# State-space branch in finer pipelined steps: half swaps on ScalarE, rotation tables on VectorE, one Toeplitz tile

## The chip, the cores and the metric

The kernel runs on one core of a Trainium2 chip. A core has five engines with a queue each: TensorE (PE: matmuls, with its weight loads PEld), VectorE (DVE), ScalarE (ACT), GpSimd (POOL) and SyncE (SP, which issues all transfers of this kernel). The metric is the device time of one execution in microseconds (us).

## The reference, cut to what matters

A decoder block on 1,024 tokens and 16 prepended ones (1,040 rows, width 1,024): one input projection, a state-space branch (S5) and a differential attention branch that are merged by gates, an output projection, and a feed-forward part with a convolution. The part that is changed computes, for 32 groups of 16 channels with 64 complex states each:

```python
x_re = jnp.einsum('blgc,gpc->blgp', ug, bb_re)
x_im = jnp.einsum('blgc,gpc->blgp', ug, bb_im)
_, _, s_re, s_im = lax.associative_scan(combine, (a_re_t, a_im_t, x_re, x_im), axis=1)
y = (jnp.einsum('blgp,gcp->blgc', s_re, c_re)
     - jnp.einsum('blgp,gcp->blgc', s_im, c_im) + d * ug)
```

The state obeys s[t] = a s[t-1] + x[t] with a complex a for each group and state.

## The kernel before, in words

Time is cut into 130 chunks (NJ) of 8 steps (CH). Inside a chunk the 8 steps are handled by matmuls: a Toeplitz matrix of the 8 lags (`Tz`, 128x128 for each group) from input to output, a matrix `VB` from input to the chunk's state, and `CL` from state to output. From chunk to chunk the state is a rotation times a decay. The rotation is taken out with tables of cosine and sine (`COS`, `SIN`, 130 columns per group), so that a real scan with the decay is left. The 32 groups go in four batches of 8 (`GB`). The 128 partitions hold 64 real and 64 imaginary parts, so turning a complex number needs a copy with the two halves exchanged (`Vs` of `Vv`, `zs` of `z`).

`ssm()` is a generator. It first computes small parameters on VectorE (three steps), and then each batch in four steps: (1) load the input `U` and the parameters, build the tables by doubling on GpSimd (`COS`, `SIN`, scratch `rot`: 8 rounds of 6 operations), and make `Z` on VectorE; (2) make `CL`, transpose `Z` into `VB`, multiply for the lag matrix `KM`, zero `Tn` on GpSimd, place `KM` into `Tn` by 8 transfers (L672), and reorder `Tn` into `Tz` by a ScalarE copy; (3) `vps = VB x U` evicted by ScalarE into `Vv`, the swap `Vs` by two transfers, turn, eight scans into `z` (L691), the swap `zs` by two transfers, turn back into `zp`; (4) `yps = CL x zp + Tz x U`, evicted and stored.

These steps are traced between the blocks of the input projection: four steps, then one before each of 12 blocks (query, key and value of four heads), and the rest (three yields) each with fillers. A block is three chunks of 348, 346 and 346 columns with 24 matmuls each. For queries and keys a norm follows: ScalarE squares the chunk into `qv` and copies it to `qraw`, and then `norm` (put into `self.later`) multiplies `qv` by a block matrix (`qss`, in the only PSUM buffer of tag `q`) and finishes on VectorE and ScalarE. `run_later` runs the waiting norms after the next chunk's matmuls.

Fillers are the 16 gate blocks and the two output matmuls of the state-space branch, handed out in items of three matmuls; an item is priced 3 x columns / 2400 us. Each of the remaining `ssm` yields takes items until PRE = 9 us are spent. What is left goes into the attention, where PE keeps the traced order and `pump(us)` calls dose the items; what remains at the end is issued at once. Gate 14 also starts `load_y`, which brings the branch's output back for its gelu.

Outside the attention the order on each engine is set when the kernel is built, by a planner that runs the instructions on a simulated time line. `keep_in_program_order(ins)` puts an instruction behind the one that was traced before it on the same engine; what is traced later may still be issued ahead of it. Each engine then works its list in order.

## Time and profile before

| | |
|---|---|
| runs | 1458.82, 1459.75, 1461.63 us (median 1459.75) |
| profiled execution | 1459.82 us, span 1458.0 us, mean granted clock 0.988 |
| PE busy | 1414.3 us (97%) |
| DVE, ACT, POOL busy | 1031.1, 613.5, 508.8 us |
| input projections with the state-space batches | about 60 to 300 us |
| attention | about 300 to 652 us |
| output projection and feed-forward | from about 652 us |

A view of waits shows for an engine's line what it waited for, the total, how often and the longest. A view of windows shows busy time in a stretch, the number of instructions, and PEclk, the clock granted to TensorE as a share of 2.4 GHz. A line can be that of a helper: L92 is `tt`, L104 is `act`, L130 and L182 are the matmuls of projections and fillers.

### The profile page before, as it was taken

To read this page: it belongs to the slowest core of one execution; us is meant where nothing else is said; L and a number is where in the kernel's file an instruction comes from. 1 tells how busy PE (TensorE), PEld (TensorE's weight loads), DVE (VectorE), ACT (ScalarE), POOL (GpSimd) and SP (SyncE) were. 2 spreads that over 40 slices of the span, in tenths; PEclk is the share of its full clock that TensorE was granted. 3 is DMA by queue.
4 is the path that set the end of the run, shared out by engine and by line. 5 is a ranking of instruction groups with operands and counts; after the bars stand their busy time and mean duration, and the time that the engine had idled before them with its cause. 6 is when DMAs were issued, how large, how long until landed. Compare 5 with 4: busy or idle time off the path is not lost.

```text
span 1458.0 us, 23036 instructions
## 1 busy us (share of the span) xinstructions
PE 1414.3 (97%) x8714; PEld 1301.7 (89%) x8714; DVE 1031.1 (71%) x1902; ACT 613.5 (42%) x1144; POOL 508.8 (35%) x453
## 2 busy tenths in 40 slices
PE   7979999999999999999999999999999999999998
PEld 7979898999999888999999899998899998788887
DVE  7958677645646869557565998888676768896574
ACT  6133343335545477443244543333333333444442
POOL 2085574511111311000122056666555566231030
PEclk9999999999999989999999999999999999999999
DMA  5424334382423523558434313334233236944331
GB/s 196 137 67 127 107 109 117 125 218 61 117 87 117 132 74 90 195 166 311 136 121 141 112 62 123 123 126 136 95 108 109 95 123 217 366 161 154 125 126 58
DMA packets 78206, 195.72 MB, mean 134 GB/s; under 512 B 9360, under 2 KB 21008, under 8 KB 78096
## 3 DMA queue, kind: packets, MB, share of 16 engines
q1 hardware_dynamic: 78096, 194.26, 41.4%
q8 instruction: 68, 1.11, 0.3%
q14 instruction: 42, 0.34, 0.1%
HBM read 133.28 MB, written 55.50 MB: 129 GB/s over the span
## 4 chain that ended last, share of the span: by engine, by line
PE 63%; DVE 15%; DMA 7%; POOL 6%; issue 4%; ACT 3%; SPq 2%; DVEq 0%; ACTq 0%; POOLq 0%
PE ps_mm L182 36%; PE ps_mm L130 20%; DVE wop L92 3%; DMA wraw<-in_w_up 2%; PE po L1401 2%; DVE u L92 1%; POOL rot L92 1%; POOL crow L92 1%; DVE crow L101 1%; DMA zs<-z 1%; POOL COS L92 1%; POOL SIN L92 1%; PE s L1365 1%; PE wt L1410 1%; PE s L1366 1%
## 5 line engine op out<-in xcount | busy, mean ns | idle before, releaser
L130 PE MATMUL ps_mm<-B,wop 128*128 128x512 f32 (+2 forms) x2772 | 438.2, 320 | 5.1 <-DVE u L92 4.2
L130 PEld LDWEIGHTS ps_mm<-B,wop 128*128 128x128 f32 x2772 | 396.3, 189 | 46.6 <-ACT wop L104 6.0
L182 PE MATMUL ps_mm<-bop,wop 128*128 128x512 f32 x924 | 214.9, 394 | 0.8 <-DVE bop L92 0.8
L182 PEld LDWEIGHTS ps_mm<-bop,wop 128*128 128x128 f32 x924 | 173.3, 188 | 42.2 <-DVE bop L92 1.7
L182 PE MATMUL ps_mm<-hhi,whi 128*128 128x342 f32 (+2 forms) x432 | 138.7, 332 | 2.9 <-ACT hhi L104 2.9
L182 PE MATMUL ps_mm<-hlo,whi 128*128 128x342 f32 (+2 forms) x432 | 139.6, 323 | 1.1 <-DVE hlo L101 1.0
L182 PE MATMUL ps_mm<-hhi,wlo 128*128 128x342 f32 (+2 forms) x432 | 139.1, 323 | 0.0
L92 POOL TENSOR_TENSOR wlo<-wraw,whi 128x1024 fp32r<-128x1024 f32 x18 | 44.7, 2486 | 205.5 <-ACT whi L104 190.1
L130 PE MATMUL ps_mm<-hhi,whi 128*128 128x348 f32 (+3 forms) x336 | 113.5, 338 | 0.0
L92 DVE TENSOR_TENSOR wop<-wraw,wop 128x512 fp32r<-128x512 f32 x88 | 91.1, 1040 | 31.4 <-ACT wop L104 30.9
L130 PE MATMUL ps_mm<-hhi,wlo 128*128 128x348 f32 (+3 forms) x336 | 111.0, 330 | 0.0
L130 PE MATMUL ps_mm<-hlo,whi 128*128 128x348 f32 (+3 forms) x336 | 111.0, 330 | 0.0
L92 POOL TENSOR_TENSOR crow<-crow,T 128x512 f32<-128x512 f32 x44 | 71.5, 1642 | 99.9 <-DVE T L92 93.2
L104 ACT ACTIVATE whi<-wraw 128x1024 fp32r<-128x1024 f32 (+3 forms) x62 | 62.1, 1003 | 99.0 <-PE ps_mm L182 39.1
L104 ACT ACTIVATE wop<-wraw 128x512 fp32r<-128x512 f32 x88 | 54.5, 628 | 115.9 <-DMA wraw<-in_w_up 49.9
L104 ACT ACTIVATE bop<-act 128x512 fp32r<-128x512 f32 x77 | 48.3, 632 | 114.4 <-PE ps_mm L182 114.2
L1367 DVE CUSTOM_DVE_ANT_0 S<-s,bias 128x348 f32<-128x348 f32 (+9 forms) x120 | 57.8, 484 | 51.6 <-PE s L1366 51.0
L92 DVE TENSOR_TENSOR bop<-act,bop 128x512 fp32r<-128x512 f32 x77 | 58.1, 756 | 45.5 <-ACT bop L104 45.5
L182 PEld LDWEIGHTS ps_mm<-hhi,whi 128*128 128x128 f32 x432 | 81.8, 191 | 3.7 <-ACT hhi L104 3.3
L92 DVE TENSOR_TENSOR wop<-S,wop 128x512 fp32r<-128x512 f32 x66 | 65.4, 991 | 27.2 <-ACT wop L104 27.1
L182 PEld LDWEIGHTS ps_mm<-hlo,whi 128*128 128x128 f32 x432 | 82.9, 192 | 2.0 <-DVE hlo L101 1.7
L104 ACT ACTIVATE wop<-S 128x512 fp32r<-128x512 f32 x66 | 41.1, 629 | 99.0 <-POOL S L92 78.8
(310 smaller groups left out, 3150.0 us busy)
## 6 DMA issues: line engine op xcount, KB each, us to landing
wraw<-in_w_up SPq DMA_DIRECT2D x49, 512.0 KB, 3.5
wraw<-in_w_in SPq DMA_DIRECT2D x30, 512.0 KB, 4.4
d_act<-crow SPq DMA_DIRECT2D x22, 512.0 KB, 3.0
act<-d_act SPq DMA_DIRECT2D x44, 256.0 KB, 3.7
wd<-in_w_down SPq DMA_DIRECT2D x22, 512.0 KB, 8.4
d_t<-T SPq DMA_DIRECT2D x33, 256.0 KB, 3.8
act<-d_t SPq DMA_DIRECT2D x33, 256.0 KB, 3.0
d_gate<-gate SPq DMA_DIRECT2D x16, 513.0 KB, 5.0
```

Source lines behind the costliest of these rows:

```text
L92: (eng or self.nc.vector).tensor_tensor(out=out, in0=in0, in1=in1, op=op)
L101: self.nc.vector.scalar_tensor_tensor(out=out, in0=in0, scalar=s, in1=in1, op0=op0, op1=op1)
L104: self.nc.scalar.activation(out, in_, func, **kw)
L130: self.nc.tensor.matmul(out=ps, lhsT=w, rhs=b, start=(i == 0), stop=(i == n - 1))
L182: self.nc.tensor.matmul(out=ps, lhsT=w, rhs=b, start=first and i == 0, stop=last and i == 2)
L1365: nc.tensor.matmul(out=ps, lhsT=q, rhs=self.KH[j][:, c0m:c0m + cm], start=True, stop=False)
L1366: nc.tensor.matmul(out=ps, lhsT=q, rhs=self.KL[j][:, c0m:c0m + cm], start=False, stop=True)
L1367: nc.vector.tensor_tensor_reduce(out=s[0:M, c0:c0 + cn], in0=ps[0:M, off:off + cn], in1=self.bias[0:M, b0 + c0:b0 + c0 + cn], scale=1.0, s ...
L1401: nc.tensor.matmul(out=po[0:M], lhsT=l, rhs=rr, start=(kk == 0), stop=(kk == nb))
L1410: nc.tensor.transpose(ps[:, r], w[:, NM + 128 * kk:NM + 128 * (kk + 1)], b.ident)
```

## The change

The tables are made by VectorE. A base of 17 columns (`CB`, `SB`, all 32 groups) is built once by five doubling rounds (`turn`); each batch copies its part and doubles on from 17 to 129 columns (`NR`) in three rounds. `Tn` and its ScalarE reorder into `Tz` are gone: one tile `toe` is zeroed once, and the 8 transfers of each batch write `KM` straight into its final layout, where a row is 8 runs of 16 numbers. The transfers that swapped halves are ScalarE copies of 64 partitions: six from PSUM (beside the eviction of `vps`), four after the scans. Scans and turns work in place in `Vv` and `Vs`. The second products of `Z` and `CL` are made and added in two halves (`more`). A batch has the steps `begin`, `lags`, `inflow`, `scan`, `back`, `outflow`; the tables of batch b+1 are traced with the scan of batch b, its lags with the outflow of batch b. Some instructions are kept behind the one traced before them (`pin`). Five steps come ahead of the first block, so that four yields are left for fillers. Norms are run one chunk later (`run_later(1)`).

```diff
@@ -24,6 +24,8 @@
+NR = NJ - 1
+BASE = 17
@@ -60,7 +62,7 @@
-        "sm": 6, "sm2": 2, "cm": 4, "xr": 11, "rot": 2, "KM": 1, "Dg": 1, "sb": 1,
+        "sm": 6, "sm2": 2, "cm": 4, "xr": 9, "rot": 2, "KM": 1, "Dg": 1, "sb": 1,
@@ -228,7 +230,7 @@
-            step(4)
+            step(5)
@@ -358,7 +360,7 @@
-            self.run_later()
+            self.run_later(1)
@@ -380,17 +382,17 @@
-    def run_later(self):
-        for f in self.later:
-            f()
-        self.later = []
+    def run_later(self, keep=0):
+        while len(self.later) > keep:
+            self.later.pop(0)()
...
-            self.run_later()
+            self.run_later(int(c0 == 0))
@@ -596,63 +598,64 @@
+        CB, SB = x.tile([128, NG, BASE], F32, name="CB"), x.tile([128, NG, BASE], F32, name="SB")
+        self.tt(CB[:, :, 0], co[:, 3 * NG:], LR[:, 0], ALU.mult)
+        self.tt(SB[:, :, 0], sis, LR[:, 0], ALU.mult)
+        ln = 1
+        while ln < BASE:
+            n = min(ln, BASE - ln)
+            self.turn(CB, SB, ln, n, NG, None)
+            ln += n
+        toe = x.tile([128, GB, CH, 16], F32, name="toe")
+        G.memset(toe, 0.0)
...
-        for b in range(4):
-            gs = slice(b * GB, (b + 1) * GB)
-            wide = lambda nm: x.tile([128, GB, NJ], F32, tag="xr", name=nm)
+        wide = lambda nm, n=NJ: x.tile([128, GB, n], F32, tag="xr", name=nm)
+        full = [128, GB, 8, 16]
+        st = [{} for _ in range(4)]
+        pin = self.tc.keep_in_program_order
+        def more(out, p, q, op):
+            for g0 in range(0, GB, 4):
+                gs = slice(g0, g0 + 4)
+                t = x.tile([128, 4, 8, 16], F32, tag="zt", name="zt")
+                self.tt(t, p[:, gs], q[:, gs], ALU.mult)
+                self.tt(out[:, gs], out[:, gs], t, op)
+        def begin(b):
+            d, gs = st[b], slice(b * GB, (b + 1) * GB)
...
-            B1, B2, C1, C2, Dd = (sb[:, i] for i in range(5))
-            cn = x.tile([128, GB, 16], F32, tag="cn", name="cn")
-            self.ts(cn, C1, sgn, ALU.mult)
-            u = wide("U")
+            d["sb"] = sb
+            u = d["u"] = wide("U")
...
-            C, S = wide("COS"), wide("SIN")
-            G.tensor_copy(C[:, :, 0], co[:, 3 * NG + b * GB:3 * NG + (b + 1) * GB])
-            G.tensor_copy(S[:, :, 0], sis[:, gs])
-            ln = 1
-            while ln < NJ:
-                n = min(ln, NJ - ln)
-                cL = C[:, :, ln - 1:ln].to_broadcast([128, GB, n])
-                sL = S[:, :, ln - 1:ln].to_broadcast([128, GB, n])
-                t1 = x.tile([128, GB, 64], F32, tag="rot", name="rot1")[:, :, 0:n]
-                t2 = x.tile([128, GB, 64], F32, tag="rot", name="rot2")[:, :, 0:n]
-                c1, s1 = C[:, :, ln:ln + n], S[:, :, ln:ln + n]
-                self.tt(c1, C[:, :, 0:n], cL, ALU.mult, eng=G)
-                self.tt(t1, S[:, :, 0:n], sL, ALU.mult, eng=G)
-                self.tt(s1, S[:, :, 0:n], cL, ALU.mult, eng=G)
-                self.tt(t2, C[:, :, 0:n], sL, ALU.mult, eng=G)
-                self.tt(c1, c1, t1, ALU.subtract, eng=G)
-                self.tt(s1, s1, t2, ALU.add, eng=G)
+            C, S = d["C"], d["S"] = wide("COS", NR), wide("SIN", NR)
+            V.tensor_copy(C[:, :, 0:BASE], CB[:, gs])
+            V.tensor_copy(S[:, :, 0:BASE], SB[:, gs])
+            ln = BASE
+            while ln < NR:
+                n = min(ln, NR - ln)
+                self.turn(C, S, ln, n, GB, None)
...
+        def lags(b):
+            d, gs = st[b], slice(b * GB, (b + 1) * GB)
+            B1, B2, C1, C2, Dd = (d["sb"][:, i] for i in range(5))
+            cn = x.tile([128, GB, 16], F32, tag="cn", name="cn")
+            self.ts(cn, C1, sgn, ALU.mult)
...
-            Zt = x.tile([128, GB, 8, 16], F32, tag="xr", name="Zt")
-            full = [128, GB, 8, 16]
...
-            self.tt(Zt, b2, gi, ALU.mult)
-            self.tt(Z, Z, Zt, ALU.add)
-            yield
-            CL = x.tile([128, GB, 8, 16], F32, tag="xr", name="CL")
-            Ct = x.tile([128, GB, 8, 16], F32, tag="xr", name="Ct")
-            c1v = C1[:, :, None, :].to_broadcast(full)
-            c2v = C2[:, :, None, :].to_broadcast(full)
-            lr = LRs[:, :, gs].rearrange("p m g -> p g m")[:, :, :, None].to_broadcast(full)
-            li = LI[:, 1:9, gs].rearrange("p m g -> p g m")[:, :, :, None].to_broadcast(full)
-            self.tt(CL, c1v, lr, ALU.mult)
-            self.tt(Ct, c2v, li, ALU.mult)
-            self.tt(CL, CL, Ct, ALU.subtract)
+            more(Z, b2, gi, ALU.add)
...
-            VB = x.tile([128, GB, 128], F32, tag="xr", name="VB")
+            VB = d["VB"] = x.tile([128, GB, 128], F32, tag="xr", name="VB")
@@ -666,51 +669,102 @@
-            Tn = x.tile([128, CH, GB, 16], F32, tag="xr", name="Tn")
-            G.memset(Tn, 0.0)
...
-                nc.sync.dma_start(out=Tn[(7 - n) * 16:128, n], in_=KM[0:(n + 1) * 16])
-            Tz = x.tile([128, GB, CH, 16], F32, tag="xr", name="Tz")
-            self.act(Tz.rearrange("p g n c -> p n g c"), Tn, AF.Copy)
-            yield
-            Vv, Vs = wide("Vv"), wide("Vs")
+                nc.sync.dma_start(out=toe[(7 - n) * 16:128, :, n], in_=KM[0:(n + 1) * 16])
+        def swap(vs, v):
+            self.act(vs[0:64], v[64:128], AF.Copy)
+            self.act(vs[64:128], v[0:64], AF.Copy)
+        def inflow(b):
+            d, gs = st[b], slice(b * GB, (b + 1) * GB)
+            Vv, Vs = d["Vv"], d["Vs"] = wide("Vv"), wide("Vs")
+            G.memset(Vv[:, :, 0:1], 0.0)
...
-                ps = self.psum("t", [128, ng, NJ], name="vps")
+                ps = self.psum("t", [128, ng, NR], name="vps")
...
-                    nc.tensor.matmul(out=ps[:, g], lhsT=VB[:, g0 + g], rhs=u[:, g0 + g], start=True, stop=True)
-                self.act(Vv[:, g0:g0 + ng], ps, AF.Copy)
-            nc.sync.dma_start(out=Vs[0:64], in_=Vv[64:128])
-            nc.sync.dma_start(out=Vs[64:128], in_=Vv[0:64])
-            self.tt(Vv, Vv, C, ALU.mult)
-            self.tt(Vs, Vs, S, ALU.mult)
-            self.tt(Vv, Vv, Vs, ALU.add)
-            z, zs = wide("z"), wide("zs")
+                    pin(nc.tensor.matmul(out=ps[:, g], lhsT=d["VB"][:, g0 + g], rhs=d["u"][:, g0 + g, 0:NR],
+                                         start=True, stop=True))
+                self.act(Vv[:, g0:g0 + ng, 1:], ps, AF.Copy)
+                swap(Vs[:, g0:g0 + ng, 1:], ps)
+            C1, C2 = d["sb"][:, 2], d["sb"][:, 3]
+            CL = d["CL"] = x.tile([128, GB, 8, 16], F32, tag="xr", name="CL")
+            c1v = C1[:, :, None, :].to_broadcast(full)
+            c2v = C2[:, :, None, :].to_broadcast(full)
+            lr = LRs[:, :, gs].rearrange("p m g -> p g m")[:, :, :, None].to_broadcast(full)
+            li = LI[:, 1:9, gs].rearrange("p m g -> p g m")[:, :, :, None].to_broadcast(full)
+            self.tt(CL, c1v, lr, ALU.mult)
+            more(CL, c2v, li, ALU.subtract)
+        def scan(b):
+            d = st[b]
+            v, vs = d["Vv"][:, :, 1:], d["Vs"][:, :, 1:]
+            pin(V.tensor_tensor(out=v, in0=v, in1=d["C"], op=ALU.mult))
+            self.tt(vs, vs, d["S"], ALU.mult)
+            self.tt(v, v, vs, ALU.add)
...
-                V.tensor_tensor_scan(out=z[:, g], data0=mag8[:, b * GB + g:b * GB + g + 1].to_broadcast([128, NJ]),
-                                     data1=Vv[:, g], initial=0.0, op0=ALU.mult, op1=ALU.add)
-            nc.sync.dma_start(out=zs[0:64], in_=z[64:128])
-            nc.sync.dma_start(out=zs[64:128], in_=z[0:64])
-            self.tt(z, z, C, ALU.mult)
-            self.tt(zs, zs, S, ALU.mult)
-            zp = x.tile([128, GB, NJ + 1], F32, tag="xr", name="zp")
-            G.memset(zp[:, :, 0:1], 0.0)
-            self.tt(zp[:, :, 1:], z, zs, ALU.subtract)
-            yield
-            y = wide("Y")
+                V.tensor_tensor_scan(out=v[:, g], data0=mag8[:, b * GB + g:b * GB + g + 1].to_broadcast([128, NR]),
+                                     data1=v[:, g], initial=0.0, op0=ALU.mult, op1=ALU.add)
+            for g0 in (0, 4):
+                swap(d["Vs"][:, g0:g0 + 4, 1:], d["Vv"][:, g0:g0 + 4, 1:])
+        def back(b):
+            d = st[b]
+            v, vs = d["Vv"][:, :, 1:], d["Vs"][:, :, 1:]
+            pin(V.tensor_tensor(out=v, in0=v, in1=d["C"], op=ALU.mult))
+            self.tt(vs, vs, d["S"], ALU.mult)
+            self.tt(v, v, vs, ALU.subtract)
+        def outflow(b):
+            d, u, y = st[b], st[b]["u"], st[b]["Vs"]
...
-                    nc.tensor.matmul(out=ps[:, g], lhsT=CL[:, g0 + g].rearrange("p n c -> p (n c)"),
-                                     rhs=zp[:, g0 + g, 0:NJ], start=True, stop=False)
-                    nc.tensor.matmul(out=ps[:, g], lhsT=Tz[:, g0 + g].rearrange("p n c -> p (n c)"),
+                    pin(nc.tensor.matmul(out=ps[:, g], lhsT=d["CL"][:, g0 + g].rearrange("p n c -> p (n c)"),
+                                         rhs=d["Vv"][:, g0 + g], start=True, stop=False))
+                    nc.tensor.matmul(out=ps[:, g], lhsT=toe[:, g0 + g].rearrange("p n c -> p (n c)"),
...
+            st[b] = None
+        begin(0)
+        yield
+        lags(0)
+        yield
+        for b in range(4):
+            inflow(b)
...
+            scan(b)
+            if b < 3:
+                begin(b + 1)
+            yield
+            back(b)
+            yield
+            outflow(b)
+            if b < 3:
+                lags(b + 1)
+            yield
+    def turn(self, C, S, ln, n, g, eng):
+        cL = C[:, :, ln - 1:ln].to_broadcast([128, g, n])
+        sL = S[:, :, ln - 1:ln].to_broadcast([128, g, n])
+        t1, t2 = (self.x.tile([128, 512], F32, tag="rot", name=nm)[:, 0:g * n].rearrange("p (g n) -> p g n", g=g)
+                  for nm in ("rot1", "rot2"))
+        c1, s1 = C[:, :, ln:ln + n], S[:, :, ln:ln + n]
+        self.tt(c1, C[:, :, 0:n], cL, ALU.mult, eng=eng)
+        self.tt(t1, S[:, :, 0:n], sL, ALU.mult, eng=eng)
+        self.tt(s1, S[:, :, 0:n], cL, ALU.mult, eng=eng)
+        self.tt(t2, C[:, :, 0:n], sL, ALU.mult, eng=eng)
+        self.tt(c1, c1, t1, ALU.subtract, eng=eng)
+        self.tt(s1, s1, t2, ALU.add, eng=eng)
```

## Rows read from the trace of the kernel before

**Rows 1.** Page: busy time, share of span, instructions of each engine.

```profile
PE 1414.3 (97%) x8714; PEld 1301.7 (89%) x8714; DVE 1031.1 (71%) x1902; ACT 613.5 (42%) x1144; POOL 508.8 (35%) x453
```

**Rows 2.** Waits of PE, whole span: total us, times, longest.

```profile
PE qss L369 <- ACT qv L104: 13.6, 3, 9.4
...
PE ot L1457 <- ACT orow L104: 3.5, 1, 3.5
...
PE yps L706 <- POOL rot L92: 1.9, 2, 1.3
```

**Rows 3.** Windows of 8 us: busy us (instructions) by engine, PEclk, DMA share, GB/s.

```profile
100.00:108.00 8.00, 1.10 (x7) 0.80 (x6) 0.00 (x0) 1.47 (x3) 3.40 (x9) 0.86 0.38 115
108.00:116.00 8.00, 5.53 (x17) 5.05 (x18) 4.48 (x7) 2.70 (x7) 0.00 (x0) 0.50 0.41 122
156.00:164.00 8.00, 6.07 (x27) 5.33 (x27) 2.79 (x5) 4.17 (x9) 3.02 (x9) 0.79 0.64 187
228.00:236.00 8.00, 5.69 (x25) 4.92 (x25) 7.50 (x15) 3.12 (x6) 0.35 (x1) 0.79 0.23 56
```

**Rows 4.** Timeline of PE, first and last of 13 matmuls in a row.

```profile
265.75 0.32 PE L182 MATMUL ps_mm<-hhi,whi 128*128 128x342 f32 x1
...
267.65 0.32 PE L182 MATMUL ps_mm<-hhi,whi 128*128 128x342 f32 x1
```

**Rows 5.** Chain that ended last, 69 to 112 us: start, us, what.

```profile
69.55 0.92 POOL COS L614
...
98.03 1.02 POOL rot L92
99.06 0.91 POOL Tn L670
...
99.98 0.62 SPq L672
...
104.46 1.93 DMA Tn<-KM
...
106.53 1.06 ACT Tz L104
...
110.07 0.36 ACT qv L104
...
110.47 1.52 PE qss L369 x2
```

**Rows 6.** Timeline of DVE, 71 to 78 us: start, us, operation.

```profile
71.49 0.41 DVE L92 TENSOR_TENSOR cm<-LI,fi 128x256 f32<-128x256 f32 x1
71.82 0.41 DVE L92 TENSOR_TENSOR cm<-LR,fi 128x256 f32<-128x256 f32 x1
...
76.25 1.23 DVE L92 TENSOR_TENSOR CL<-sb,LRs 128x1024 f32<-128x1024 f32 x1
77.40 1.23 DVE L92 TENSOR_TENSOR Ct<-sb,LI 128x1024 f32<-128x1024 f32 x1
```

**Rows 7.** Windows: VectorE's full stretch, the whole stage, two parts of the attention.

```profile
44.00:84.00 40.00, 40.00 (x257) 39.57 (x255) 39.59 (x136) 7.15 (x13) 14.45 (x18) 1.00 0.36 115
60.00:300.00 240.00, 224.20 (x1416) 216.72 (x1415) 168.73 (x289) 87.45 (x177) 136.29 (x215) 0.96 0.37 109
500.00:540.00 40.00, 35.96 (x208) 33.63 (x207) 31.24 (x67) 23.67 (x44) 8.76 (x7) 0.87 0.20 62
633.00:650.00 17.00, 16.70 (x111) 14.47 (x110) 7.59 (x27) 8.77 (x31) 0.00 (x0) 1.00 0.64 207
```

**Rows 8.** Groups of ACT: count, busy us, mean ns, idle before and releaser.

```profile
L104 ACT ACTIVATE wt<-wt 16x128 f32<-16x128 f32 (+5 forms) x84 | 29.4, 381 | 18.5 <-PE wt L1412 11.0 <-PE wt L1410 6.9
...
L104 ACT ACTIVATE yz<-yz 128x520 f32<-128x520 f32 x8 | 5.1, 632 | 14.0 <-DVE yz L101 14.0
...
L104 ACT ACTIVATE Vv<-vps 128x390 f32<-128x390 f32 (+1 forms) x12 | 4.7, 451 | 0.0
...
L104 ACT ACTIVATE Tz<-Tn 128x1024 f32<-128x1024 f32 x4 | 4.2, 1059 | 25.1 <-DMA Tn<-KM 25.1
```

## The prediction

> **What bounds the kernel now.** I read the page first: TensorE is busy for 97% of the span and its weight loads for 89% [rows 1]. So a change of the state-space branch can win no more than the time in which TensorE waits for that branch or runs at a lower clock because of it. The list of TensorE's waits shows how much this is [rows 2]: `qss` waited 13.6 us for ScalarE's `qv`, in three pieces (one of 9.4 us), and `yps` 1.9 us. The releaser named for `yps` is a GpSimd table operation, but the matmul reads `zp`, which VectorE ends just then; the late thing is the turn back. That is 15.5 us of idle time in the stage. A third wait, `ot` for 3.5 us, lies in the attention and comes back below.
>
> The windows show what comes on top [rows 3]. After a stall the granted clock is 0.50 of 2.4 GHz for a while, that is 1.2 GHz. At full clock 12 matmul steps take 1.90 us, 0.158 us each [rows 4]. From 108 to 116 us TensorE was busy for 5.53 us with 17 matmuls, which is 2.7 us of work: 2.8 us lost. From 156 to 164 us it is 6.07 less 27 x 0.158, 1.8 us, and from 228 to 236 us 5.69 less 25 x 0.158, 1.7 us. Together 6.3 us. All that the stage can give is therefore 15.5 + 6.3 = 21.8 us.
>
> The chain of waits says why the big stall exists [rows 5]. GpSimd builds the tables of the first batch from 69.55 to 99.06 us; behind them in its queue it zeroes `Tn` (0.91 us); then SyncE issues eight transfers of about 0.6 us each; the last lands 1.93 us later; ScalarE copies `Tz` (1.06 us), evicts `Vv`, and works off an older norm before it reaches the `qv` for which TensorE stands. The copy of `Tz` sits at the head of ScalarE's queue and waits 25.1 us in four times [rows 8], and the squares of the projection wait behind it. It is not the transfer that is long; it is a slow engine's list ahead of it, which the planner took for shorter.
>
> **The change part by part.** The profiled execution took 1459.82 us (span 1458.0), 0.07 above the median of the runs, so I sum against 1459.8 and correct nothing.
>
> *GpSimd's tables and the `Tz` copy go.* This takes away the cause of the three `qss` stalls: ScalarE no longer waits for a chain of GpSimd and transfers. What is late next on ScalarE is a swap that waits for VectorE's scans. Behind it stand again the squares of a chunk; but the norms now run one chunk later, and a chunk is 24 matmuls, 24 x 0.158 = 3.8 us. So TensorE has one more chunk of cover: by this alone the smaller stalls (1.9 to 2.3 us) would be gone even if ScalarE were as late as before, and the large one would fall from 9.4 to 5.6 us.
>
> *VectorE takes the tables.* From start to start a 256-column operation takes 0.33 us and a 1,024-column one 1.15 us [rows 6]; that is 0.057 us plus 1.07 ns a column. The base has rounds of 32, 64, 128, 256 and 32 columns, six operations each: 6 x 0.83 = 5.0 us. A batch has rounds of 136, 272 and 488 columns, 6 x 1.13 = 6.8 us, and two copies of at most 0.2 us: 7.2 us, 28.7 us for four. Halving the second products costs two more fixed parts in each of two places, 0.24 us a batch, 1.0 us. Sum 34.7 us on VectorE. In the stage it is now busy for 168.7 of 240 us, 70% [rows 7]; it would be at 203. If the stage shrinks by 21.8 us and takes in 10.4 us of fillers (below), that is 203 of 229 us, 89%. There is room, but little: this is the term I trust least. The first tables end earlier even so. The base and the first batch take 12 us of VectorE where GpSimd took 29 us [rows 5].
>
> *ScalarE takes the swaps.* Six copies from PSUM a batch at the 0.451 us of the `Vv` eviction, four of 516 columns at 0.632 us [rows 8], less one `Tz` of 1.06 us: 2.7 + 2.5 - 1.1 = 4.2 us a batch, 17 us in all. ScalarE goes from 87 to about 104 us of the stage, under half. I cost this at nothing; the cover is its idle time.
>
> *SyncE and transfers.* Sixteen swap transfers go. The eight of `KM` stay. In the old order they stood ahead of stores and of the next weights; now they can wait for the `yps` matmuls of the batch before, because there is only one `toe`, and what is behind them in SyncE's list waits too (weight loads above all). They are traced right behind those matmuls, and their reader comes three blocks (some 36 us) later, so I cost this at nothing. Their runs become 64 bytes long instead of 512, eight times as many; no row shows such runs. From below they land in 1.93 us [rows 5], from above in eight times that, 15 us each. Both are within 36 us, so the sum takes nothing for it.
>
> The Trainium skill's "DMA: Bandwidth & Descriptors" (Specifications) asks for at least 512 bytes for the full rate; its "Why small descriptors are slow (HBM only)" says that transfers inside SBUF, as these are, don't pay. No row here tells which holds; by the first the third rival below is the case, by the second nothing changes.
>
> *Matmuls.* The same number, with one column fewer in 130 for `vps`: nothing.
>
> *Fillers move.* Three yields were left for fillers, now four are. One yield takes items of 3 x 342 / 2400 = 0.4275 until 9 are spent: 22 items, 66 matmuls, 10.4 us of TensorE. They leave the attention, where I counted the pump calls: they can take some 457 items, before there were 528 - 66 = 462 and now 440. So fillers ran out just at the end and now run out 17 items early. These are 51 matmuls, 8.1 of the 16.7 busy us between 633 and 650 us [rows 7]. There each block goes from TensorE to ScalarE and back (eviction `wt`, 0.381 us [rows 8], two for each of the last three blocks), with nothing to fill the gaps. The cost is nothing if all gaps fall under other work, and 8 us if the stretch doesn't shorten. Six evictions are 2.3 us and a little for the hand-overs: I take 3.
>
> *The attention's worst place shifts.* From 500 to 540 us TensorE idles 4.0 us, and the clock is at 0.87 [rows 7]. There the branch's gelu falls on the change of heads; `ot` waits 3.5 us for ScalarE [rows 2], whose gelu steps `yz` wait for VectorE 14.0 us in all [rows 8]. Fillers run 22 of 462 items ahead after the change, some 17 of the attention's 352 us, so the two meet differently. It could vanish (4 us idle and 40 x 0.13 = 5 us of clock) or grow by as much; I take nothing.
>
> *Sum.* Of the stage's 21.8 us I leave one stall of the size seen from 228 to 236 us (2.3 us idle and 1.7 us of clock), since VectorE at 89% will be late somewhere. 1459.8 - 21.8 + 4.0 + 3 = 1445.0 us.
>
> **The rivals.** *VectorE becomes the bound in part.* For: 89%, and from 44 to 84 us it is busy for nearly all of the time already [rows 7], where 12 us more now belong. Against: in just that stretch TensorE is busy throughout. If half of the gain is lost, 1459.8 - 10.9 + 3 = 1452 us, up to 1457.
>
> *Slower: VectorE frees the `qss` bank late.* There is one buffer of tag `q`. A `qss` must wait until VectorE has read the one before, and behind a waiting `qss` all matmuls stand. If VectorE runs more than a chunk (3.8 us) behind, every chunk of queries and keys pays. At 24 chunks the point of decision is 21.8 / 24 = 0.9 us a chunk; with 1.5 us and a clock that falls with each, as the small stalls show (1.7 us each), in half of them, it is 24 x 1.5 + 12 x 1.7 = 56 us against 21.8: about 1490; just past the point 1463 to 1475. For: VectorE's load. Against: in the list of TensorE's waits `qss` stands for ScalarE alone [rows 2].
>
> *Small packets, and no gain.* If the eight transfers take 15 us and not 1.93, a weight load behind them lands 13 us later. With two chunks (7.6 us) of cover TensorE waits 5.5 us in three batches and loses 1.7 us of clock with each, 21.6 us: the gain is gone, 1460 to 1463 us.
>
> *Better than thought.* The collision in the attention goes as well: 1445 - 9 = 1436 us, or 1432 with no stall left in the stage.
>
> **How the numbers follow.** My forecast, with 1438 (all of the stage's 21.8 us) to 1452, gets 0.64; VectorE in part (1452 to 1457) 0.14; the slower case 0.10; no gain, by packets or by a stall that moved, 0.05; better than 1438 0.07. The likeliest is 1445. From 1437 to 1457 holds some 0.8, as the slower case and half of the better one stay outside. A change of 0.2% (3 us) is about what a measurement of this kernel tells from none. Faster by more than that: 0.64 + 0.14 + 0.07, less a little at the edge, 0.84; within 0.06; slower 0.10.
>
> **What would show it.** Right: in the waits of TensorE `qss` on `qv` is nearly gone, PEclk is 1.00 from 100 to 250 us, VectorE is near 200 us in the stage, GpSimd near nothing, and the attention starts some 10 us earlier although it begins after 22 more items. The last 17 us before the output projection have more gaps. Wrong: TensorE waits for VectorE (`q` bank, weights' low parts), ScalarE sits in a swap before `qv`, or SyncE in a `KM` transfer before a weight load; or a new stall where gelu and heads meet eats the gain.

## The result and the profile after

The changed kernel took 1439.67 us in the median of 4 runs (1438.4 to 1441.15), the kernel before 1459.94 (1458.82 to 1461.63) beside it: a ratio of 0.9858, 95% interval 0.984 to 0.9876, some 20.3 us faster. The forecast was 1445.0, with a range from 1437 to 1457. The profiled execution took 1438.99 us. Its busy time, from the page, answers to [rows 1] (in this kernel the helpers stand two lines later: L94 is `tt`, L106 is `act`, L132 and L184 are the matmuls):

```profile
PE 1407.9 (98%) x8714; PEld 1298.4 (90%) x8714; DVE 1051.0 (73%) x2030; ACT 630.8 (44%) x1180; POOL 379.7 (26%) x250
```

GpSimd lost 129 us of work, and VectorE gained only 20. TensorE's waits over the whole span, against [rows 2]:

```profile
PE s L1419 <- DVE m L1421: 5.8, 3, 4.1
...
PE po L1455 <- ACT wt L106: 2.5, 5, 0.7
PE ps_mm L184 <- DVE gate L94: 2.1, 1, 2.1
...
PE ps_mm L132 <- ACT wop L106: 0.8, 1, 0.8
```

`qss` and `yps` are gone from the list, and so is `ot`; what stands at its head is the attention's `s`. The windows, the small ones against [rows 3] and the large ones against [rows 7]:

```profile
100.00:108.00 8.00, 8.00 (x51) 7.80 (x50) 8.00 (x17) 4.03 (x9) 0.00 (x0) 1.00 0.54 107
108.00:116.00 8.00, 8.00 (x53) 8.00 (x52) 8.00 (x22) 4.33 (x9) 0.00 (x0) 1.00 0.52 173
156.00:164.00 8.00, 8.00 (x51) 7.79 (x50) 8.00 (x20) 4.41 (x7) 0.00 (x0) 1.00 0.36 132
...
60.00:300.00 240.00, 240.00 (x1561) 234.95 (x1560) 191.44 (x423) 115.92 (x222) 8.29 (x13) 1.00 0.40 113
460.00:500.00 40.00, 35.62 (x217) 33.22 (x218) 36.77 (x75) 27.59 (x46) 15.02 (x11) 0.91 0.51 127
500.00:540.00 40.00, 37.88 (x241) 35.92 (x240) 29.89 (x87) 25.68 (x72) 4.96 (x3) 0.96 0.24 74
```

In the stage TensorE now works for all of the 240 us at full clock, with 145 matmuls more than before, also where VectorE is busy without a break (8.00 of 8.00). The attention begins 13.3 us earlier (first `vt` at 305.73, before at 319.06 us) although the 22 fillers of 10.4 us now come ahead of it: 23.7 us won until there. From there to the first matmul on `mhi` it takes 371.7 us where it took 379.7: 8.0 less for the 10.4 us of work that left, 2.4 us lost. Behind that, in the output projection and the feed-forward part, nothing changes: 759.7 us to the end, before 759.3.

The timeline of TensorE, GpSimd and VectorE at the attention's new worst place shows one chain (the wait is in brackets):

```profile
464.00 0.66 PE L1419 MATMUL s<-KH,QQ 128*128 128x348 f32 x1 [4.13 <-DVE m L1421]
...
461.98 1.53 DVE L103 SCALAR_TENSOR_TENSOR yz<-yz,yt 128x520 f32<-128x520 f32 x1 [4.91 <-POOL yz L94]
...
460.89 2.06 POOL L94 TENSOR_TENSOR yz<-yt 128x520 f32<-128x520 f32 x2 [7.95 <-DMA yt<-d_y]
```

### The profile page after: what moved, and what is told of

Its sections match the earlier page's. It is cut to its first block, busy times and chain, and to the rows that moved or that the text cites. A ratio compares the mean times of both kernels' runs of the same rounds, so it can differ in the third digit from the quotient of the medians.

```text
span 1437.2 us, 22951 instructions
## 1 busy us (share of the span) xinstructions
PE 1407.9 (98%) x8714; PEld 1298.4 (90%) x8714; DVE 1051.0 (73%) x2030; ACT 630.8 (44%) x1180; POOL 379.7 (26%) x250
## 4 chain that ended last, share of the span: by engine, by line
PE 76%; DVE 10%; DMA 5%; POOL 4%; issue 3%; ACT 2%; SPq 1%; DVEq 0%; ACTq 0%; POOLq 0%
PE ps_mm L184 38%; PE ps_mm L132 28%; PE po L1455 3%; DMA wraw<-in_w_up 2%; DVE wop L94 2%; POOL crow L94 2%; DVE crow L103 1%; PE s L1419 1%; PE wt L1464 1%; PE s L1420 1%; PE qss L371 1%; POOL S L94 1%; DVE u L94 1%; DMA wd<-in_w_down 1%; DMA yt<-d_y 1%
## 5 line engine op out<-in xcount | busy, mean ns | idle before, releaser
L132 PE MATMUL ps_mm<-B,wop 128*128 128x512 f32 (+2 forms) x2772 | 436.6, 319 | 4.3 <-DVE u L94 3.4
L132 PEld LDWEIGHTS ps_mm<-B,wop 128*128 128x128 f32 x2772 | 395.2, 189 | 45.3 <-ACT wop L106 5.2
L184 PE MATMUL ps_mm<-bop,wop 128*128 128x512 f32 x924 | 216.0, 395 | 2.6 <-DVE bop L94 2.6
L184 PEld LDWEIGHTS ps_mm<-bop,wop 128*128 128x128 f32 x924 | 174.1, 189 | 44.4 <-DVE bop L94 3.5
L184 PE MATMUL ps_mm<-hhi,whi 128*128 128x342 f32 (+2 forms) x432 | 138.0, 330 | 1.9 <-ACT hhi L106 1.9
L184 PE MATMUL ps_mm<-hlo,whi 128*128 128x342 f32 (+2 forms) x432 | 139.6, 323 | 0.1
L184 PE MATMUL ps_mm<-hhi,wlo 128*128 128x342 f32 (+2 forms) x432 | 139.5, 324 | 0.0
L106 ACT ACTIVATE whi<-wraw 128x1024 fp32r<-128x1024 f32 (+3 forms) x62 | 62.1, 1003 | 133.2 <-PE ps_mm L184 53.6
L94 DVE TENSOR_TENSOR wop<-wraw,wop 128x512 fp32r<-128x512 f32 x88 | 98.0, 1119 | 23.6 <-ACT wop L106 23.2
L132 PE MATMUL ps_mm<-hhi,whi 128*128 128x348 f32 (+3 forms) x336 | 111.9, 333 | 0.2 <-ACT rms_u L106 0.2
L132 PE MATMUL ps_mm<-hhi,wlo 128*128 128x348 f32 (+3 forms) x336 | 109.7, 326 | 0.0
L132 PE MATMUL ps_mm<-hlo,whi 128*128 128x348 f32 (+3 forms) x336 | 108.8, 324 | 0.0
L94 POOL TENSOR_TENSOR wlo<-wraw,whi 128x1024 fp32r<-128x1024 f32 x18 | 44.6, 2477 | 214.1 <-ACT whi L106 211.9
L94 DVE TENSOR_TENSOR wop<-S,wop 128x512 fp32r<-128x512 f32 x66 | 64.9, 983 | 48.1 <-ACT wop L106 48.1
L106 ACT ACTIVATE bop<-act 128x512 fp32r<-128x512 f32 x77 | 48.4, 632 | 117.3 <-PE ps_mm L184 117.3
L94 POOL TENSOR_TENSOR crow<-crow,T 128x512 f32<-128x512 f32 x44 | 70.6, 1618 | 96.3 <-DVE T L94 90.8
L106 ACT ACTIVATE wop<-wraw 128x512 fp32r<-128x512 f32 x88 | 54.1, 626 | 93.2 <-DMA wraw<-in_w_up 51.6
L94 DVE TENSOR_TENSOR bop<-act,bop 128x512 fp32r<-128x512 f32 x77 | 60.1, 781 | 44.0 <-ACT bop L106 43.9
L106 ACT ACTIVATE wop<-S 128x512 fp32r<-128x512 f32 x66 | 40.4, 626 | 109.5 <-POOL S L94 98.8
L184 PEld LDWEIGHTS ps_mm<-hhi,whi 128*128 128x128 f32 x432 | 81.2, 190 | 3.1 <-ACT hhi L106 2.5
L184 PEld LDWEIGHTS ps_mm<-hlo,whi 128*128 128x128 f32 x432 | 83.0, 192 | 0.8 <-DVE hlo L103 0.6
```

Source lines behind the costliest of these rows:

```text
L94: (eng or self.nc.vector).tensor_tensor(out=out, in0=in0, in1=in1, op=op)
L106: self.nc.scalar.activation(out, in_, func, **kw)
L132: self.nc.tensor.matmul(out=ps, lhsT=w, rhs=b, start=(i == 0), stop=(i == n - 1))
L184: self.nc.tensor.matmul(out=ps, lhsT=w, rhs=b, start=first and i == 0, stop=last and i == 2)
```

## The experiments

All intervals are of the ratio to the kernel before, which ran beside each. The theory at the start: ScalarE's copy `Tz`, which waits for GpSimd and eight transfers at the head of its queue, makes `qss` late. The rivals: the place of the tables, the cover by the later norms, VectorE's load.

### The direct Toeplitz tile alone

The kernel before, with this edit (and one buffer of `xr` fewer, for room):

```diff
+        toe = x.tile([128, GB, CH, 16], F32, name="toe")
+        G.memset(toe, 0.0)
         yield
...
-            Tn = x.tile([128, CH, GB, 16], F32, tag="xr", name="Tn")
-            G.memset(Tn, 0.0)
             for n in range(CH):
-                nc.sync.dma_start(out=Tn[(7 - n) * 16:128, n], in_=KM[0:(n + 1) * 16])
-            Tz = x.tile([128, GB, CH, 16], F32, tag="xr", name="Tz")
-            self.act(Tz.rearrange("p g n c -> p n g c"), Tn, AF.Copy)
+                nc.sync.dma_start(out=toe[(7 - n) * 16:128, :, n], in_=KM[0:(n + 1) * 16])
```

> The kernel before with one part of the change: the transfers write the Toeplitz tile directly, and GpSimd's zeroing for each batch and ScalarE's copy of the tile go. If the copy at the head of ScalarE's queue is what made qss wait (my theory), the 13.6 us of qss waits and the 6.3 us of lower clock behind them go, and the 1.9 us of yps stays or grows: 1440 to 1445 us. If the slow tables on GpSimd are the cause (the rival), only the wait moves from qss to yps, which now waits for the transfers and the turn back itself: 1452 us or more. If the cover by the later norms is what counts, 1455 us or more.

Measured: 0.9933 (0.9911 to 0.9955), half of the gain and between the two expectations. TensorE's waits in the stage, and VectorE's:

```profile
PE ps_mm L130 <- DVE vrow L92: 4.8, 1, 4.8
...
PE yps L704 <- POOL rot L92: 1.5, 2, 0.8
...
DVE Vv L92 <- POOL COS L92: 7.2, 1, 7.2
```

All `qss` waits are gone, as the theory says. But the wait moved: VectorE now stands 7.2 us for GpSimd's first table with the evictions queued behind it, and TensorE 4.8 us for one of them (`vrow`). The copy was the place where the lateness showed, and one half of its price.

### The later norms alone, and with the direct tile

The kernel before, with `self.run_later()` as `self.run_later(1)` in the queries' and keys' chunks (and the first chunk of values); then the same edit on top of the direct tile.

> The kernel before with the norms of a chunk run one chunk later and nothing else. By the prediction's working one more chunk is 3.8 us of cover: the small qss waits (some 2 us each, with 1.7 us of clock each) go, the one of 9.4 us falls to about 5.6 us: 1448 to 1452 us. If the order of the norms hides nothing, since the copy of the Toeplitz tile blocks ScalarE for all of them in any case: 1458 to 1461 us.

Measured: 1.0080 (1.0066 to 1.0093), slower by 12 us. Neither expectation holds.

> The kernel before with the direct Toeplitz tile and the norms one chunk later, both together; tables stay on GpSimd and swaps stay transfers. Alone the first gave 0.9933 and the second 1.0080 of the time before. If the later norms hurt whenever the branch's tables come late, because VectorE then stands in the branch with the norms behind it, the two together give 1455 us or more. If they hurt only beside the copy that blocks ScalarE, they help here: 1440 to 1446 us.

Measured: 0.9925 (0.9905 to 0.9946), no different from the direct tile alone and between the two expectations. TensorE's waits of the norms alone, and one with the direct tile:

```profile
PE qss L369 <- DVE qv L101: 9.8, 2, 8.2
PE yps L706 <- DVE zp L92: 5.9, 1, 5.9
PE yps L706 <- POOL rot L92: 5.9, 3, 3.3
```

```profile
PE qss L369 <- DVE qv L101: 6.2, 2, 4.4
```

The big wait fell from 9.4 to 8.2 us, not to 5.6, and its releaser changed: no longer ScalarE's `qv`, but VectorE's, which frees the one `qss` bank. VectorE had itself stood 11.2 us for ScalarE's `qu`, which stood behind the copy `Tz` (11.7 us): the same late chain, met through the bank. The waits of `yps` grew from 2.2 to 11.8 us, 5.9 of them in one piece at the last batch. There the eight scans took 4.82 us in place of 2.67, because one of them lasted as long as an operation of GpSimd that had started just before it (in the kernel before all 32 scans took 0.40 to 0.43 us):

```profile
293.34 2.53 POOL L92 TENSOR_TENSOR wlo<-wraw,whi 128x1024 fp32r<-128x1024 f32 x1 [10.22 <-ACT whi L104]
293.59 2.56 DVE L691 TENSOR_TENSOR_SCAN z<-ex_e,Vv 128x130 f32<-128x130 f32 x1
```

That is 2.2 of the 5.9 us; the growth of the other `yps` waits was not traced. A chunk of cover is worth nothing while the chain behind is late by more. About 2 of the 12 us had been lost before the first chunk of queries (the weights' copy there ran at 65.87 us, before at 63.72).

### The norms at their old place in the changed kernel

The changed kernel with `self.run_later()` at both places.

> The changed kernel with the norms at their old place, one chunk earlier. If ScalarE is never late any more, the extra chunk of cover is not used: 1439 to 1441 us. If the cover is what keeps TensorE busy while VectorE is full (from 60 to 124 us in the trace), qss waits come back: 1445 us or more.

Measured: 0.9927 (0.9915 to 0.9939), 10 us of the gain lost. Here, where nothing else is late, the cover counts, though of the `qss` waits that were expected only 0.5 us came back. TensorE's waits in the stage:

```profile
PE yps L728 <- DVE Vv L94: 2.3, 1, 2.3
...
PE qss L371 <- ACT qv L106: 0.5, 1, 0.5
```

These 2.8 us with the clock (0.99 in the stage) and a later start make 6.5 us until the first `mhi`, which begins at 683.92 us against 677.47. The other 5.4 us lie behind it, where the source of the two kernels is the same: 765.1 us against 759.7. The GpSimd tables below show 765.2 there and the direct tile alone 762.7, all others lie between 757.5 and 759.9. Of the 5.4 us, 4.3 are longer waits of TensorE for VectorE's `u` and `bop` in the feed-forward part (6.7 and 3.6 us, in the changed kernel 3.4 and 2.6); what makes VectorE later there was not found. So the cover is worth some 6 us by this trace, and 10 at most.

### GpSimd's tables in the changed kernel

```diff
-            self.turn(CB, SB, ln, n, NG, None)
+            self.turn(CB, SB, ln, n, NG, G)
...
-                self.turn(C, S, ln, n, GB, None)
+                self.turn(C, S, ln, n, GB, G)
```

> The changed kernel with its rotation tables, base and batches, made by GpSimd. If the place of the tables doesn't matter once no copy on ScalarE waits for them: 1438 to 1442 us, VectorE some 30 us less busy in the stage. If GpSimd's slow chain was itself the cause, the first turn waits for it, ScalarE's swaps behind the scan and the squares behind the swaps: qss or yps waits of several us again, 1445 to 1455 us.

Measured: 1.0018 (1.0004 to 1.0033). The whole gain is gone, more than expected. TensorE's waits in the stage and one of VectorE:

```profile
PE qss L371 <- DVE qv L103: 5.5, 4, 2.3
PE yps L728 <- DVE Vv L94: 4.2, 1, 4.2
...
DVE COS L636 <- POOL CB L94: 5.0, 1, 5.0
```

Of the 24 us between the profiled spans of the two kernels, 18.6 are lost before the first `mhi` and 5.5 behind it, in the part whose lengthening is unexplained above. `qss` waits for VectorE four times, because its bank comes free late. The longest of these waits (2.3 us, at 88 us) follows the 5.0 us in which VectorE stood for GpSimd's base tables. Ahead of the other three, 3.2 us together, VectorE had no such stand, and why its `qv` was late there was not traced. That is the mechanism of the prediction's slower rival; at the first of the four it was started by VectorE's standing still and not by its load.

### VectorE's tables in the kernel before

```diff
-            G.tensor_copy(C[:, :, 0], co[:, 3 * NG + b * GB:3 * NG + (b + 1) * GB])
+            V.tensor_copy(C[:, :, 0], co[:, 3 * NG + b * GB:3 * NG + (b + 1) * GB])
...
-                self.tt(c1, C[:, :, 0:n], cL, ALU.mult, eng=G)
+                self.tt(c1, C[:, :, 0:n], cL, ALU.mult)
```

and so for the other copy and the other five operations.

> The kernel before with one part of the change: the rotation tables of each batch are made by VectorE, in the old rounds from one column up; the zeroing and the copy of the Toeplitz tile, the transfers and the norms stay. If the cause of the big qss wait is that GpSimd's list ahead of the zeroing is slow (29 us for the first tables, most of it because an operation of GpSimd waits for one of VectorE beside it), the copy on ScalarE comes on time and 10 to 20 us are gained: 1440 to 1450 us, with VectorE some 38 us of operations fuller and its other operations shorter again. If the copy at the head of ScalarE's queue costs by itself, whoever makes the tables, the qss waits stay: 1455 us or more.

Measured: 0.9885 (0.9871 to 0.9898), as the first expectation has it: 16.8 of the 20.7 us that the changed kernel's ratio is worth, by this part alone. The waits of ScalarE and of TensorE in the stage:

```profile
ACT Tz L104 <- DMA Tn<-KM: 9.6, 4, 4.9
...
PE qss L369 <- ACT qv L104: 0.2, 1, 0.2
```

The copy is still there and still waits, but 9.6 us instead of the 25.1 of [rows 8], and TensorE hardly sees it. With GpSimd nearly idle (9.5 of the 240 us), VectorE's other operations are shorter too. Its groups of the stage (mean ns of one), first with the tables on GpSimd (the direct tile alone), then with VectorE's tables:

```profile
L92 DVE TENSOR_TENSOR wlo<-wraw,whi 128x1024 fp32r<-128x1024 f32 x15 | 20.1, 1339 | 2.2 <-ACT whi L104 2.1
L101 DVE SCALAR_TENSOR_TENSOR qy<-qu,qy 128x346 f32<-128x346 f32 x16 | 12.1, 757 | 0.5
L92 DVE TENSOR_TENSOR qu<-qu,qv 128x346 f32<-128x346 f32 x16 | 10.9, 678 | 7.8 <-ACT qu L104 7.8
...
L101 DVE SCALAR_TENSOR_TENSOR qv<-qss,E 128x346 f32<-128x346 f32 x16 | 8.2, 513 | 9.5 <-PE qss L369 9.5
```

```profile
L92 DVE TENSOR_TENSOR wlo<-wraw,whi 128x1024 fp32r<-128x1024 f32 x15 | 18.3, 1219 | 1.8 <-ACT whi L104 1.8
...
L92 DVE TENSOR_TENSOR qu<-qu,qv 128x346 f32<-128x346 f32 x16 | 8.2, 512 | 3.7 <-ACT qu L104 3.6
L101 DVE SCALAR_TENSOR_TENSOR qy<-qu,qy 128x346 f32<-128x346 f32 x16 | 8.2, 510 | 0.2
L101 DVE SCALAR_TENSOR_TENSOR qv<-qss,E 128x346 f32<-128x346 f32 x16 | 8.2, 509 | 1.1 <-PE qss L369 1.1
```

In these groups the operations with both inputs in SBUF are 10 to 48% longer when GpSimd makes the tables; the one that reads PSUM (`qv`) is not.

### Work on GpSimd that nobody needs

The changed kernel, with multiplications behind the small zeroing of each batch, 60 a batch, then 30:

```diff
             G.memset(Vv[:, :, 0:1], 0.0)
+            junk = x.tile([128, 3, NG], F32, tag="gj", name="gj")
+            for _ in range(60):
+                self.tt(junk, GR[:, 0:3], GI[:, 0:3], ALU.mult, eng=G)
```

> The changed kernel with idle work put on GpSimd: in each of the four batches 60 multiplications of two small tables into a scratch tile that nothing reads, some 27 to 36 us a batch, about as long as GpSimd worked on the tables before. No other engine waits for it. If GpSimd's work costs time because VectorE's operations with two inputs in SBUF take longer beside it (346 columns: 511 ns in the changed kernel, 575 to 754 ns in the kernels with tables on GpSimd), VectorE's mean for qy, qu, qraw and wlo rises again and 4 to 10 us of the gain are lost: 1443 to 1450 us. If GpSimd's work cost time only because its tables came late for the others, 1438 to 1441 us.

Measured: 1.0305 (1.0281 to 1.0329), 66 us lost against the changed kernel, far outside both. The list was too long: the zeroing of the next batch stood behind it, and `yps` waited 58.6 us for it.

> The changed kernel with half of the idle work on GpSimd, 30 operations a batch. With 60 the list was not done when the small zeroing behind it was due, and that is where the 66 us went (yps waited 58.6 us for it), so this run keeps the list shorter than the time to the next zeroing: at 0.87 us each, as measured, 26 us a batch. If GpSimd beside VectorE costs the others only through GpSimd's own late results, nothing waits now: 1438 to 1442 us, with GpSimd's 96 columns still near 0.9 us in the mean beside 0.44 us alone. If VectorE's lengthened operations cost by themselves: 1444 us or more.

Measured: 1.0134 (1.0116 to 1.0152). Half of the work still costs 40 us. The time lies in the second range, but not by its mechanism: VectorE's operations were hardly longer (`qy` 525 ns, `qu` 546, `wlo` 1213, in the changed kernel 511, 511 and 1216). The reason is the finding. TensorE's wait, and four windows (columns as in [rows 3]):

```profile
PE yps L731 <- POOL Vv L683: 34.7, 2, 25.1
```

```profile
76.00:84.00 8.00, 8.00 (x49) 7.59 (x49) 8.00 (x27) 3.50 (x7) 7.24 (x3) 1.00 0.20 65
100.00:108.00 8.00, 8.00 (x54) 7.80 (x53) 8.00 (x18) 4.20 (x11) 7.77 (x4) 1.00 0.39 90
148.00:156.00 8.00, 8.00 (x62) 7.55 (x61) 3.89 (x7) 4.88 (x12) 6.83 (x16) 1.00 0.18 74
196.00:204.00 8.00, 0.00 (x0) 0.00 (x0) 0.00 (x0) 0.00 (x0) 6.67 (x18) 0.50 0.00 0
```

GpSimd does 18 of these operations in 8 us when VectorE is idle, and 3 or 4 when VectorE is busy throughout. TensorE and ScalarE are not what slows it: from 148 to 156 us TensorE is busy throughout and ScalarE for more than half, VectorE for less than half, and 16 are done. The timeline has two that took 19.75 us together, one of them 12.16:

```profile
110.86 19.75 POOL L94 TENSOR_TENSOR gj<-GR,GI 128x96 f32<-128x96 f32 x2
```

So the list ends when VectorE's pauses let it. The 32 operations ahead of the second batch's zeroing took 67 us (from 76.6 to 143.6); at the idle pace they would have taken 12. That made the first of TensorE's two waits, 9.7 us. The second, 25.1 us, has one more cause: ahead of the third batch's zeroing stood 88 operations and not 30, as the planner had moved the idle work of the later batches there. The run did not keep the list as short as it was meant to, and some 30 a batch were tested in the first wait alone. GpSimd's work cost others only through its own late result (the small zeroing).

The tables of the kernel before show the same. An operation of the same shape took 1.19 us beside VectorE's operations of 1,024 columns [rows 6] and 0.23 us later, while VectorE stood idle (97.8 to 110.1 us):

```profile
76.36 1.19 POOL L92 TENSOR_TENSOR COS<-COS 128x16 f32<-128x16 f32 x1
...
102.19 0.23 POOL L92 TENSOR_TENSOR COS<-COS 128x16 f32<-128x16 f32 x1
```

The Trainium skill's "SBUF — State Buffer" (Who interferes with whom) says that VectorE and GpSimd share a port pair under an exclusive lock, that a VectorE instruction with two SBUF inputs contends with a GpSimd instruction that reads SBUF, and that the order of issue decides which of the two blocks. The traces agree on who is touched (`qy` 757 against 510 ns, `qv` from PSUM 513 against 509), and the scan of 2.56 us above is a case in which GpSimd came first. One thing differs: the longest VectorE instruction while that GpSimd operation took 12.16 us lasted 1.22 us, so GpSimd was not let in after one instruction of VectorE. That VectorE, busy without a break, holds GpSimd to about a fifth of its pace is the run's own number.

### The tables twice on VectorE

The rounds of each batch in the changed kernel stand in `for _ in range(2):`.

> The changed kernel with each batch's tables built twice on VectorE, the same values: 27 us more work for VectorE in the stage. If the 48 us in which VectorE is idle there (240 less 191) are room, 1439 to 1443 us. If VectorE is as good as the bound, as the prediction's first rival says, nearly all of it is paid: 1455 to 1467 us.

Measured: 0.9874 (0.9852 to 0.9896), 1442.32 us. VectorE is busy for 213.35 of the 240 us, 22 more than in the changed kernel, and TensorE waits for 1.9 us of the stage:

```profile
60.00:300.00 240.00, 238.07 (x1538) 232.74 (x1537) 213.35 (x496) 111.74 (x218) 6.26 (x12) 0.99 0.38 106
```

```profile
PE ps_mm L132 <- DVE vrow L94: 1.9, 1, 1.9
```

The difference of the ratios, 0.0016 or 2.3 us, lies within the intervals. Most of the 27 us found room. But the trace shows one stall, 1.9 us for `vrow`, with a granted clock of 0.93 around it (172 to 196 us), which is 24 x 0.07 = 1.7 us, and the attention begins 5.8 us later than in the changed kernel.

### Swaps by transfers

```diff
-            self.act(vs[0:64], v[64:128], AF.Copy)
-            self.act(vs[64:128], v[0:64], AF.Copy)
+            nc.sync.dma_start(out=vs[0:64], in_=v[64:128])
+            nc.sync.dma_start(out=vs[64:128], in_=v[0:64])
```

Each swap is then called once on the whole tile, behind the evictions and behind the scans.

> The changed kernel with the half swaps done by transfers again, two for a swap as before, and not by ScalarE copies. By the prediction this part is worth nothing by itself: 1438 to 1442 us. If the swap's own time matters, because VectorE waits for it with the norms queued behind (in the kernel before VectorE waited 19.1 us for the swaps, in the changed one 2.4 us), some 17 us more idle time falls on a VectorE that has 48 us to spare: 1444 to 1452 us.

Measured: 0.9846 (0.9823 to 0.9868): the swaps on ScalarE bring nothing. VectorE waits 7.3 us for the transfers, which its room covers; TensorE waits for nothing in the stage.

### Fewer fillers ahead of the attention, and earlier transfers

`PRE` of 7.0 instead of 9.0; and, in another kernel, `self.load_y()` at gate `YGATE - 1` with the gelu left at `YGATE`.

> The changed kernel with 17 filler items at each of the four places instead of 22: 68 before the attention, about the 66 of the kernel before. By the prediction's term the tail of the attention gets its 17 to 20 items back and 2 to 3 us with them: 1436 to 1438 us. If the place of the gelu in the attention counts for more than the tail, it moves back by some 15 us of the attention, and the sign is open: 1434 to 1444 us. If neither counts, 1439 to 1440 us.

Measured: 0.9849 (0.9832 to 0.9865), 1437.72 us.

> The changed kernel with the 32 transfers that bring the branch's result back issued one gate block (24 items) earlier than the gelu on it, and nothing else moved. In the changed kernel the gelu's first operation on VectorE waits 4.9 us for GpSimd, that waits 8.0 us for these transfers, and the attention's exponents behind it make TensorE wait 4.1 us. If the transfers are the late link, this wait and the clock behind it go: 1432 to 1437 us. If the gelu's own chain over three engines is what costs, 1438 to 1441 us.

Measured: 0.9847 (0.9833 to 0.986), 1436.97 us. Both lie 1.3 to 1.6 us below the changed kernel by their ratios, inside the intervals: no version was found that measurably beats it. With fewer fillers the four waits of `po` at the attention's end (0.17 to 0.65 us each, 1.9 together) are gone from the trace, two thirds of the prediction's 3 us. With earlier transfers the gelu itself began 25 us earlier, and GpSimd waited for the transfers as long as ever:

```profile
435.76 2.06 POOL L94 TENSOR_TENSOR yz<-yt 128x520 f32<-128x520 f32 x2 [8.02 <-DMA yt<-d_y]
```

The planner moved both. TensorE's longest wait there fell from 4.1 to 2.5 us, but `po` waited 6.0 us in nine places for ScalarE.

## Why the prediction was right, point by point

- *The stall and its clock.* "All that the stage can give is therefore 15.5 + 6.3 = 21.8 us": the attention's start shows 23.7 us, with about 0.9 won ahead of the stage. This term was right to 1 us.
- *The residual stall, 4.0 us, is the mis-sized term: it measured 0.* I kept it because VectorE would be at 89%, "the term I trust least". The load was wrong, not the stall that belongs to it: VectorE is busy for 191.4 of the 240 us, 80%. Its page time grew by 19.9 us, not by 34.7, mostly because its other operations are shorter without GpSimd's tables beside them: from the kernel before to the changed one `wlo`, `qraw`, `qu` and `qy` are shorter by 2.9, 4.0, 2.2 and 2.3 us in the first 300 us, 11.4 together. (The page's total also holds shifts elsewhere, such as 7 us more for `wop` in the feed-forward part.) At 89%, where the doubled tables are, TensorE did stall once, 1.9 us and 1.7 of clock, about the 4.0 us that I held back; even so the run's time was no more than 2.3 us longer, within the noise.
- *The cause.* "A slow engine's list ahead of it, which the planner took for shorter" is borne out by the tables alone, 16.8 us. Why the list is slow the prediction did not see, though [rows 5] and [rows 6] lie beside each other: GpSimd was held up by VectorE's operations. Summed over the durations of the same 200 operations, the tables took 137 us on GpSimd in the kernel before and 57 us on VectorE in the run that moved only them; with the shortest duration of each shape GpSimd would have taken some 78 us, which is an estimate from the same trace. (The first batch's tables end at 102.2 us, not at 99.06: two of their operations run behind the zeroing.) The two main parts alone give 16.8 and 9.8 us, more than the 20.7 us of the whole change; that both shorten one chain is the likely reason and was not tested by a run with these two alone.
- *The norms.* "By this alone the smaller stalls would be gone ..., and the large one would fall from 9.4 to 5.6 us" is wrong: alone they cost 12 us, and they pay 6 to 10 us only where the chain behind is no longer late. The cover was counted in matmuls; but `qss` then met its bank, which VectorE freed late behind the same copy.
- *Swaps, small packets.* Both at nothing, and both rightly. From issue to landing the median transfer of `toe` took 2.2 us (1.9 to 4.3; of `Tn` before 1.9), where 1.93 and 15 were the bounds. Of the two sections of the Trainium skill's "DMA: Bandwidth & Descriptors" that the prediction weighed, the trace agrees with "Why small descriptors are slow (HBM only)".
- *Fillers.* 3 us for the tail; 2.4 us are lost from the attention to `mhi`, 1.9 of them the four waits of `po`. *The collision* at nothing: it moved from 500 to 464 us and kept its size (`ot` 3.5 us before, `s` 4.1 now; 464 matmuls from 460 to 540 us before, 458 now). The terms as measured, -13.3 until the attention, -8.0 from there to `mhi` and +0.5 behind, make -20.8, by which the profiled span fell.

Of the rivals, VectorE as the bound and the small packets are refuted; the late `qss` bank is a real mechanism that the changed kernel doesn't meet, but that the later norms beside GpSimd's tables do (9.8, 6.2 and 5.5 us in three runs). That rival's own terms add up to 1497 us (1459.8 - 21.8 + 56.4 + 3), where about 1490 stands.

## What to carry to other kernels

Elementwise work on GpSimd beside a busy VectorE is not a second pair of hands: it got on mainly in VectorE's pauses and could lengthen VectorE's own operations, so moving it to VectorE can cost that engine little more than half of what it seems (by the page 19.9 us here, where 34.7 were estimated). Where an in-order queue waits at its head, look for what makes the releaser late before removing the waiting instruction. A deeper cover and an earlier result are not additive: test the cover again once the late chain is gone.

## What was not expected of the hardware

A GpSimd multiplication of 96 columns took 0.37 us from start to start beside an idle VectorE (18 in 6.67 us) and 2 to 4 us in the mean of a window of 8 us, once 12.16 us, beside one that was busy throughout. In the other direction the price varied: VectorE's groups with two SBUF inputs were 10 to 48% longer while GpSimd made the tables and 3 to 13% longer beside the small multiplications (`qy` 525 and 570, `qu` 546 and 578 ns, in the changed kernel 511). The group `qv`, which reads PSUM, was unchanged (513 against 509 ns). One scan of 0.40 us took 2.56 us behind a GpSimd operation that had started first.
